# One layer of a YOCO trunk on one core: split products for the first two projections and the output projection, a paired block solve, 32 bytes of padding, and an inverse square root formed on DVE

## The chip, the cores and the metric

The kernel runs on one core of a Trainium2 chip. The metric is the device time of one execution in microseconds; a kernel's time is the median of its runs. TensorE is called PE, VectorE DVE, ScalarE ACT, GpSimd POOL, SyncE SP.

## The reference

One sequence of 512 tokens (S), width 1024 (D), float32 throughout. Layer 0 is an RWKV-7 mixer and a SwiGLU FFN, layer 1 differential attention with a shared K and V and a second FFN. Only the mixer's computation is touched by the change:

```python
h  = rms_norm(x, g_mix[0]);  hh = shift(h) - h
xr, xw, xk, xv, xa, xg = (h + hh * mu[i] for i in range(6))
r, k, v = xr @ w_r, xk @ w_k, xv @ w_v
w = -softplus(-(w0 + tanh(xw @ w1) @ w2)) - 0.5
a = sigmoid(a0 + (xa @ a1) @ a2);   g = sigmoid(xg @ g1) @ g2
kk = k * k_k, per head of 64:  kk / max(sqrt(sum(kk*kk)), 1e-12)
k  = k * (1 + (a - 1) * k_a)
# per head, over 512 tokens:
state = state * decay_t + (state @ -kk_t) (kk_t * a_t)^T + v_t k_t^T ;  y_t = state @ r_t
y  = groupnorm(y) * lnx_w + lnx_b + (sum(r*k*r_k)) * v
x  = x + (y * g) @ w_o
x  = x + (silu(gate) * up) @ w_down      # the FFN
```

## The kernel before

The residual stream is kept transposed: tiles of 128 features by 512 tokens. There are two ways to multiply in float32. `proj_f` gives float32 operands to PE as they are; such a product of 128x128 by 128x512 stands in the trace as two MATMUL records. `mm3` takes operands split into a high part (rounded to float32r by a copy on ACT) and a low part (the rest, a subtraction on DVE), and adds up three float32r products, high by high, high by low and low by high; each is one record. Before the change the mixer uses the first way and the two FFNs and the attention the second.

The mixer is cut into 16 heads, handled as 8 pairs in two halves of four (w = 0 and 1), and into 8 chunks of 64 tokens. It runs in this order.

- The opening merges four streams: the normalised input, the two low-rank projections w1 and a1 (`lora`, L339), and the first half of r (`r_half(0)`, L459 and L174). Each of them mixes its own input (`mix_tile`, L329): one ACT instruction at L335, one DVE instruction at L336, into a tile of tag `xm` that has two buffers; k's mixes go into `xk` and are kept for the second half. Weights come through `load_raw` into tag `wr`, which has three buffers, of which w1 and a1 hold two here.
- Then `k_half(0)` is drained alone.
- After that `plan` emits three streams in the order of planned times (the table TIMES: start, end and a bend of each). The first is `pairs(0)`, `solve(0)`, `rec(0)`; the second r, k, v, the gate and the output projection of half 0; the third `pairs(1)`, `solve(1)`, `rec(1)`. `plan` sets the order in which instructions are written down. [...]
- `pairs` begins with `norms` (L498): the sums of squares of the keys by PE (L507), a clamp on DVE (L512), `rsqrt` (L200: the power of minus one half on POOL at L206, then a Newton step of three DVE instructions, L208 to L210), a transpose on PE (L515) and a copy (L517). `pair_b` needs the result.
- `solve` (L660) inverts 64x64 triangular blocks: 31 steps of two DVE instructions (L673, L675), then the off-diagonal 32x32 blocks by PE: 16 products (L695), a copy on ACT (L696), 16 products (L699), a copy (L700), for two groups (q) by two heads (par) one after the other.
- `rec` runs the recurrence over 8 chunks (L724, L738, L766 on PE, copies and sums on DVE between them); the stream of projections fills PE meanwhile. `head_out` finishes each 128 tokens.
- The second half of the output projection, `out(1)`, is drained alone after the plan. Then the first FFN begins.

SBUF pools lie on a stack from the left; the pool `z` (six tiles of 8 KB per partition), and after it `xa` (eight tiles of 4 KB), lie at the right end. In the built program the tiles of `z` and `xa` begin 32 bytes past a multiple of 64 (`xa` at 196576, 200672 and so on), those of `xb`, `hid`, `xk`, `s` and `wr` at a multiple of 64. `xa` holds the moving operand of the first FFN's gate and up products and, later, of the attention's output projection; `xb` holds that of the second FFN. `s` is a tag of 13 tiles of 4 KB that most intermediate results of the mixer share.

Of the kernel before, what the change touches and what calls it, by code (L numbers as in the profile page):

```python
# [18 lines left out]
P = 128  # L19
D = 1024  # L20
S = 512
# [21 lines left out]
class Trunk:  # L43
# [3 lines left out]
                 gate=(153, 181, 1.0), out0=(181.0, 252.922016661, 1.25), pairs1=(65, 130, 1.0), solve1=(132.962208526, 188.90025602, 1.0))  # L47
# [138 lines left out]

    def proj_tok(self, W, xgen, evac):
# [12 lines left out]
    def rsqrt(self, out, m, tag="ty"):  # L200
# [9 lines left out]
        nc.vector.scalar_tensor_tensor(out=out, in0=z, scalar=1.5, in1=y, op0=ALU.add, op1=ALU.mult)  # L210

# [55 lines left out]
    def build(self):  # L267
        tc, nc, A = self.tc, self.nc, self.A
        self.tags = {}
        with ExitStack() as st:  # L270
# [16 lines left out]
            nc.vector.memset(self.mhalf, -0.5)  # L287
            banks = dict(ca=2, cb=2, pj=4)
# [170 lines left out]
    def r_half(self, w):  # L459
        for i in range(2):  # L460
            self.R[w * 2 + i] = self.T("s", [P, 2, S])
        return self.proj_f(self.A["w_r"], self.mixes("r", 0, w),
                           lambda o, ps: self.nc.scalar.copy(self.R[o // 2][:, o % 2, :], ps), gi=w)

    def k_half(self, w, kr):
        kr.extend(self.T("s", [P, 2, S]) for _ in range(2))
        return self.proj_f(self.A["w_k"], self.mixes("k", 2, w),
# [30 lines left out]
    def norms(self, q):  # L498
# [14 lines left out]
        self.rsqrt(inv[:, :, 0:8], m, "nv")  # L513
# [39 lines left out]
    def out_half(self, w, pg, x1):  # L553

        nc, A = self.nc, self.A
        yx = {}

        def ev(o, ps):
            yx[o] = self.T("xk", [P, S])
            nc.vector.tensor_tensor(out=yx[o], in0=ps, in1=self.oT[o // 2][:, o % 2, :], op=ALU.mult)  # L560
        self.lora2(pg, [A["g2a"], A["g2b"]], w, ev)
# [5 lines left out]
        for gi in range(2):  # L567
            yield from self.proj_f(A["w_o"], lambda kt: yx[kt], add, kts=range(w * 4, w * 4 + 4), gi=gi)
# [91 lines left out]
    def solve(self, w, Ld, N2):  # L660
# [28 lines left out]
        for q in range(2):  # L689
            ln = slice(q * 16, q * 16 + 16)  # L690
            for par in range(2):
                b0, b1 = slice(par * C, par * C + 32), slice(par * C + 32, par * C + 64)
                ps = self.bank("ca")
                for l in range(16):
                    nc.tensor.matmul(ps[b1, l * 32:l * 32 + 32], N2[b0, q * 16 + l, :], Td[b0, q * 16 + l, :], start=True, stop=True)  # L695
                nc.scalar.copy(Zt[b1, ln, :], ps[b1, :].rearrange("p (a b) -> p a b", a=16))  # L696
                ps2 = self.bank("cb")
                for l in range(16):
                    nc.tensor.matmul(ps2[b0, l * 32:l * 32 + 32], Zt[b1, q * 16 + l, :], Pd[b1, q * 16 + l, :], start=True, stop=True)  # L699
                nc.scalar.copy(Ps[q][b0, :, 32:64], ps2[b0, :].rearrange("p (a b) -> p a b", a=16))  # L700
                yield
# [465 lines left out]
```

## Time and profile before

| | |
|---|---|
| median of 3 runs | 1576.84 us (1575.41 to 1577.22) |
| the profiled execution | 1575.47 us, its span 1573.7 us |
| PE busy | 1501.3 us, 95% of the span |
| DVE, ACT, POOL busy | 729.5, 497.9, 219.5 us |
| mean granted PE clock | 0.98 |
| opening of the mixer (four merged streams) | about 27 to 83 us |
| k's first half | about 90 to 117 us |
| the plan | about 117 to 532 us |
| second half of the output projection | about 532 to 562 us |
| first FFN, attention, second FFN | about 562 to 1574 us |

The bounds of the stages are read from the order of PE's instructions in time. A busy PE is not a PE at its peak: records of matmuls overlap, so a rate is read from the distance of their starts.

### The profile page before, as it was taken

To read this page: it belongs to the slowest core of one execution; us is meant where nothing else is said; L and a number is where in the kernel's file an instruction comes from. 1 tells how busy PE (TensorE), PEld (TensorE's weight loads), DVE (VectorE), ACT (ScalarE), POOL (GpSimd) and SP (SyncE) were. 2 spreads that over 40 slices of the span, in tenths; PEclk is the share of its full clock that TensorE was granted. 3 is DMA by queue.
4 is the path that set the end of the run, shared out by engine and by line. 5 is a ranking of instruction groups with operands and counts; after the bars stand their busy time and mean duration, and the time that the engine had idled before them with its cause. 6 is when DMAs were issued, how large, how long until landed. Compare 5 with 4: busy or idle time off the path is not lost.

```text
span 1573.7 us, 22664 instructions
## 1 busy us (share of the span) xinstructions
PE 1501.3 (95%) x9448; PEld 1124.0 (71%) x9448; DVE 729.5 (46%) x1356; ACT 497.9 (32%) x881; POOL 219.5 (14%) x182
## 2 busy tenths in 40 slices
PE   3898998999999999999999998999999999999999
PEld 1244654666567468888888888988877888888887
DVE  6313638566423453343432357666666434434232
ACT  3332340212311142222221243356564333222211
POOL 0004313201201121111110003211101111111000
PEclk9999999999898999999999998999999999999999
DMA  3121432484420222222222231221011222222231
GB/s 113 41 87 57 169 130 91 162 294 163 170 95 20 77 95 94 94 94 94 95 94 94 98 108 68 92 70 43 29 51 68 99 103 94 94 101 100 95 120 67
DMA packets 51799, 154.21 MB, mean 98 GB/s; under 512 B 5488, under 2 KB 12016, under 8 KB 49648
## 3 DMA queue, kind: packets, MB, share of 16 engines
q1 hardware_dynamic: 50496, 151.18, 27.4%
q8 instruction: 74, 1.21, 0.3%
q10 hardware_dynamic: 1120, 1.32, 0.3%
q14 instruction: 29, 0.24, 0.1%
q0 software_dynamic: 80, 0.26, 0.0%
HBM read 131.77 MB, written 20.97 MB: 97 GB/s over the span
## 4 chain that ended last, share of the span: by engine, by line
PE 81%; DVE 9%; POOL 3%; issue 2%; ACT 2%; DMA 2%; ACTq 0%; SPq 0%; POOLq 0%; DVEq 0%
PE pj L158 12%; PE pj L157 12%; PE pj L156 12%; PE pj L182 10%; PE pj L195 2%; PE d L943 2%; PE d L945 2%; PE d L944 2%; PE cb L642 2%; PE cb L766 2%; PE ca L724 1%; POOL ty L206 1%; PE pj L363 1%; PE ca L157 1%; PE cb L157 1%
## 5 line engine op out<-in xcount | busy, mean ns | idle before, releaser
L150 ACT CAST wh<-wr 128x1024 fp32r<-128x1024 f32 x153 | 160.8, 1052 | 501.8 <-PE pj L157 226.2
L151 DVE TENSOR_TENSOR wl<-wr,wh 128x1024 fp32r<-128x1024 f32 x153 | 186.9, 1222 | 184.5 <-ACT wh L150 182.9
L156 PE MATMUL pj<-xa,wh 128*128 128x512 f32 x352 | 139.9, 397 | 1.0 <-ACT wh L150 1.0
L158 PE MATMUL pj<-xa,wl 128*128 128x512 f32 x352 | 139.6, 397 | 0.3 <-DVE wl L151 0.3
L157 PE MATMUL pj<-xa,wh 128*128 128x512 f32 x352 | 139.6, 397 | 0.0
L158 PE MATMUL pj<-xb,wl 128*128 128x512 f32 x352 | 137.1, 389 | 0.0
L156 PE MATMUL pj<-xb,wh 128*128 128x512 f32 x352 | 137.1, 389 | 0.0
L157 PE MATMUL pj<-xb,wh 128*128 128x512 f32 x352 | 137.0, 389 | 0.0
L833 POOL TENSOR_TENSOR hid<-ev,hid 128x512 fp32r<-128x512 f32 x44 | 68.1, 1548 | 405.5 <-ACT hid L832 405.5
L182 PE MATMUL pj<-xk,wr 128*128 128x512 f32 x256 | 123.8, 631 | 0.0
L829 DVE TENSOR_TENSOR ev<-pj,bc 128x512 f32<-128x512 f32 x44 | 30.4, 691 | 145.2 <-PE pj L158 145.2
L206 POOL TENSOR_TENSOR ty<-ty,mhalf 128x8 f32<-128x8 f32 (+1 forms) x28 | 47.6, 1699 | 306.0 <-DVE ty L782 150.0
L182 PEld LDWEIGHTS pj<-xk,wr 128*128 128x128 f32 x256 | 48.6, 199 | 53.8 <-issue 50.6
L826 DVE TENSOR_TENSOR ev<-pj,bc 128x512 f32<-128x512 f32 x44 | 30.4, 691 | 118.6 <-PE pj L158 116.1
L156 PEld LDWEIGHTS pj<-xa,wh 128*128 128x128 f32 x352 | 66.3, 188 | 18.2 <-ACT wh L150 2.2
L158 PEld LDWEIGHTS pj<-xa,wl 128*128 128x128 f32 x352 | 66.3, 188 | 16.8 <-DVE wl L151 0.7
L157 PEld LDWEIGHTS pj<-xa,wh 128*128 128x128 f32 x352 | 66.3, 188 | 16.0
L157 PEld LDWEIGHTS pj<-xb,wh 128*128 128x128 f32 x352 | 66.1, 188 | 13.9
L158 PEld LDWEIGHTS pj<-xb,wl 128*128 128x128 f32 x352 | 66.1, 188 | 13.7
L156 PEld LDWEIGHTS pj<-xb,wh 128*128 128x128 f32 x352 | 66.1, 188 | 13.6
L158 PE MATMUL pj<-hid,wl 128*128 128x512 f32 x176 | 68.5, 389 | 0.0
L156 PE MATMUL pj<-hid,wh 128*128 128x512 f32 x176 | 68.5, 389 | 0.0
(284 smaller groups left out, 2969.6 us busy)
## 6 DMA issues: line engine op xcount, KB each, us to landing
wr<-in_wgu SPq DMA_DIRECT2D x88, 512.0 KB, 3.5
wr<-in_wdn SPq DMA_DIRECT2D x44, 512.0 KB, 3.5
st_d<-z SPq DMA_DIRECT2D x16, 1024.0 KB, 4.7
z<-st_d SPq DMA_DIRECT2D x16, 1024.0 KB, 5.8
wr<-in_w_kv SPq DMA_DIRECT2D x16, 512.0 KB, 3.5
wr<-in_w_r SPq DMA_DIRECT2D x8, 512.0 KB, 3.5
wr<-in_w_k SPq DMA_DIRECT2D x8, 512.0 KB, 3.5
wr<-in_w_v SPq DMA_DIRECT2D x8, 512.0 KB, 3.5
```

Source lines behind the costliest of these rows:

```text
L150: nc.scalar.copy(hi, raw)
L151: nc.vector.tensor_tensor(out=lo, in0=raw, in1=hi.bitcast(F32), op=ALU.subtract)
L156: mm(out, wh, xh, start=start, stop=False)
L157: mm(out, wh, xl, start=False, stop=False)
L158: mm(out, wl, xh, start=False, stop=stop)
L182: self.nc.tensor.matmul(pss[i], w[:, kt % 2, i * P:i * P + P], x, start=kt == kts[0], stop=kt == kts[-1])
L195: self.nc.tensor.matmul(pss[tt], x[:, tt * P:(tt + 1) * P], w[:, kt % 2, :], start=kt == 0, stop=kt == KT - 1)
L206: nc.gpsimd.tensor_tensor(out=y, in0=m, in1=half.to_broadcast(shp), op=ALU.pow)
L642: nc.tensor.matmul(ps[f, o:o + P], BK[f, hf * 4 + c2 * 2 + c, u, :], Z[f, c2 * 2 + c, 0:2, :].rearrange("p a b -> p (a b)"), start=True, s ...
L766: nc.tensor.matmul(ps[o, i * C:(i + 1) * C], z[f, i, k, :], R[f, i, :], start=n == 0, stop=n == len(parts) - 1)
L833: nc.gpsimd.tensor_tensor(out=t[:, 1, :], in0=b, in1=t[:, 0, :].bitcast(F32), op=ALU.subtract)
L943: mm(ps[:, t], x[:, 0, :], hi, start=kt == 0, stop=False)
```

## The change

1. `r_half(0)` and `k_half(0)` go through a new function `proj_p`: weights and mixed inputs are split, into tiles of tag `z`, and multiplied with `mm3`. The second halves stay as they are.
2. `out_half` splits the gated output and the weights of w_o and uses `mm3`. The high parts take tiles of tag `s`, the low parts of tags `xk` and `wr`.
3. `norms` calls a new function `rsqrt_v`: a first guess from the bits by two DVE instructions and three Newton steps of three DVE instructions each; POOL's power is gone from there. `rsqrt` itself stays where else it is called.
4. The end of `solve` makes the products of both heads in turn within one loop, 32 to a bank, first all of L695's kind for q = 0 and 1, then all of L699's kind; of the two copies after each one goes to ACT and one to DVE.
5. In TIMES the gate moves from 153-181 to 172-190, and out0's start from 181.0 to 190.5.
6. A pool of 32 bytes is opened on the right before all others there, so `z` and `xa` begin 32 bytes lower.

```diff
--- before.py
+++ after.py
@@ -44,7 +44,7 @@
 
     TIMES = dict(pairs0=(-0.3, 60.1, 1.0), solve0=(60.8, 109.3, 0.8), rec0=(110, 180, 1.0), rec1=(194.0, 252.732477142, 1.0),
                  r1=(-4.9, 29.584587539, 1.0), k1=(30, 58.813540184, 0.9), v0=(60.0, 97.9, 1.0), v1=(99.712791157, 150.1, 1.0),
-                 gate=(153, 181, 1.0), out0=(181.0, 252.922016661, 1.25), pairs1=(65, 130, 1.0), solve1=(132.962208526, 188.90025602, 1.0))
+                 gate=(172, 190, 1.0), out0=(190.5, 252.922016661, 1.25), pairs1=(65, 130, 1.0), solve1=(132.962208526, 188.90025602, 1.0))
 
 
     START = 8, 7.5, 7.5, 8
@@ -184,6 +184,27 @@
                     evac(gi * 4 + i, pss[i])
             yield
 
+    def proj_p(self, W, xgen, evac, gi=0):
+
+        nc = self.nc
+        pss = [self.bank() for _ in range(4)]
+        for kt in range(KT):
+            if kt % 2 == 0:
+                w = self.load_raw(W[gi, kt // 2], [P, 2, 512])
+                wz, xz = (self.T("z", [P, 4, 512], F32R) for _ in range(2))
+                nc.scalar.copy(wz[:, 0:2, :], w)
+                nc.vector.tensor_tensor(out=wz[:, 2:4, :], in0=w, in1=wz[:, 0:2, :].bitcast(F32), op=ALU.subtract)
+            x = xgen(kt)
+            k = kt % 2
+            nc.scalar.copy(xz[:, k, :], x)
+            nc.vector.tensor_tensor(out=xz[:, 2 + k, :], in0=x, in1=xz[:, k, :].bitcast(F32), op=ALU.subtract)
+            for i in range(4):
+                c = slice(i * P, i * P + P)
+                self.mm3(pss[i], wz[:, k, c], wz[:, 2 + k, c], xz[:, k, :], xz[:, 2 + k, :], kt == 0, kt == KT - 1)
+                if kt == KT - 1:
+                    evac(gi * 4 + i, pss[i])
+            yield
+
     def proj_tok(self, W, xgen, evac):
 
         pss = [self.bank() for _ in range(NT)]
@@ -208,6 +229,20 @@
         nc.vector.tensor_tensor(out=z, in0=y, in1=y, op=ALU.mult)
         nc.vector.scalar_tensor_tensor(out=z, in0=z, scalar=-0.5, in1=m, op0=ALU.mult, op1=ALU.mult)
         nc.vector.scalar_tensor_tensor(out=out, in0=z, scalar=1.5, in1=y, op0=ALU.add, op1=ALU.mult)
+
+    def rsqrt_v(self, out, m, tag):
+
+        nc = self.nc
+        I32 = mybir.dt.int32
+        shp = list(m.shape)
+        y = self.T(tag, shp)
+        nc.vector.tensor_scalar(y.bitcast(I32), m.bitcast(I32), 1, None, op0=ALU.logical_shift_right)
+        nc.vector.tensor_scalar(y.bitcast(I32), y.bitcast(I32), -1.0, float(0x5F3759DF), op0=ALU.mult, op1=ALU.add)
+        z = self.T(tag, shp)
+        for i in range(3):
+            nc.vector.tensor_tensor(out=z, in0=y, in1=y, op=ALU.mult)
+            nc.vector.scalar_tensor_tensor(out=z, in0=z, scalar=-0.5, in1=m, op0=ALU.mult, op1=ALU.mult)
+            nc.vector.scalar_tensor_tensor(out=out if i == 2 else y, in0=z, scalar=1.5, in1=y, op0=ALU.add, op1=ALU.mult)
 
     def rows_bc(self, rstd, tag="ev"):
 
@@ -285,6 +320,8 @@
             nc.vector.memset(self.zero, 0.0)
             self.mhalf = cp.tile([P, 1], F32, name="mhalf")
             nc.vector.memset(self.mhalf, -0.5)
+            self.open(st, "pad", dict(pad=1), side="right")
+            self.T("pad", [P, 8])
             banks = dict(ca=2, cb=2, pj=4)
             with ExitStack() as ps:
                 self.open(ps, "ps0", banks, space=PSUM)
@@ -459,12 +496,12 @@
     def r_half(self, w):
         for i in range(2):
             self.R[w * 2 + i] = self.T("s", [P, 2, S])
-        return self.proj_f(self.A["w_r"], self.mixes("r", 0, w),
+        return (self.proj_f if w else self.proj_p)(self.A["w_r"], self.mixes("r", 0, w),
                            lambda o, ps: self.nc.scalar.copy(self.R[o // 2][:, o % 2, :], ps), gi=w)
 
     def k_half(self, w, kr):
         kr.extend(self.T("s", [P, 2, S]) for _ in range(2))
-        return self.proj_f(self.A["w_k"], self.mixes("k", 2, w),
+        return (self.proj_f if w else self.proj_p)(self.A["w_k"], self.mixes("k", 2, w),
                            lambda o, ps: self.nc.scalar.copy(kr[o // 2 - 2 * w][:, o % 2, :], ps), gi=w)
 
     def v_half(self, w):
@@ -510,7 +547,7 @@
         nc.gpsimd.memset(inv, 0.0)
         m = self.T("nv", [P, 4, 8])
         nc.vector.tensor_scalar(m, ps[:, 0:32].rearrange("p (a b) -> p a b", a=4), 1e-24, None, op0=ALU.max)
-        self.rsqrt(inv[:, :, 0:8], m, "nv")
+        self.rsqrt_v(inv[:, :, 0:8], m, "nv")
         pt = self.bank("cb")
         nc.tensor.transpose(pt[:, 0:P], inv.rearrange("p a b -> p (a b)"), self.ident)
         it = self.T("it", [P, P])
@@ -553,11 +590,17 @@
     def out_half(self, w, pg, x1):
 
         nc, A = self.nc, self.A
-        yx = {}
+        yx, yh, yl = {}, {}, {}
 
         def ev(o, ps):
             yx[o] = self.T("xk", [P, S])
             nc.vector.tensor_tensor(out=yx[o], in0=ps, in1=self.oT[o // 2][:, o % 2, :], op=ALU.mult)
+            if o % 2 == 0:
+                yh[o // 2] = self.T("s", [P, 2, S], F32R)
+            h = yh[o // 2][:, o % 2, :]
+            nc.scalar.copy(h, yx[o])
+            yl[o] = self.T("xk", [P, S], F32R)
+            nc.vector.tensor_tensor(out=yl[o], in0=yx[o], in1=h.bitcast(F32), op=ALU.subtract)
         self.lora2(pg, [A["g2a"], A["g2b"]], w, ev)
         yield
 
@@ -565,7 +608,20 @@
             v = x1[o // 2][:, o % 2, :]
             nc.vector.tensor_tensor(out=v, in0=ps, in1=v, op=ALU.add)
         for gi in range(2):
-            yield from self.proj_f(A["w_o"], lambda kt: yx[kt], add, kts=range(w * 4, w * 4 + 4), gi=gi)
+            pss = [self.bank() for _ in range(4)]
+            for kt in range(w * 4, w * 4 + 4):
+                k = kt % 2
+                if k == 0:
+                    W = self.load_raw(A["w_o"][gi, kt // 2], [P, 2, 512])
+                    wh, wl = self.T("s", [P, 2, 512], F32R), self.T("wr", [P, 2, 512], F32R)
+                    nc.scalar.copy(wh, W)
+                    nc.vector.tensor_tensor(out=wl, in0=W, in1=wh.bitcast(F32), op=ALU.subtract)
+                for i in range(4):
+                    c = slice(i * P, i * P + P)
+                    self.mm3(pss[i], wh[:, k, c], wl[:, k, c], yh[kt // 2][:, k, :], yl[kt], k == 0 and kt % 4 == 0, kt % 4 == 3)
+                    if kt % 4 == 3:
+                        add(gi * 4 + i, pss[i])
+                yield
 
     def done_list(self, tiles):
         for j in range(KT):
@@ -686,19 +742,27 @@
                                         self.cst[:, C_RM + b:C_RM + b + 1], None, op0=ALU.mult)
             Ps.append(pt)
         Zt = self.T("s", [P, 32, 32])
-        for q in range(2):
-            ln = slice(q * 16, q * 16 + 16)
-            for par in range(2):
-                b0, b1 = slice(par * C, par * C + 32), slice(par * C + 32, par * C + 64)
-                ps = self.bank("ca")
-                for l in range(16):
+        B = [[slice(par * C + b * 32, par * C + b * 32 + 32) for par in range(2)] for b in range(2)]
+        v = lambda t: t.rearrange("p (a b) -> p a b", a=16)
+
+        def first(q):
+            ps = self.bank("ca")
+            for l in range(16):
+                for b0, b1 in zip(*B):
                     nc.tensor.matmul(ps[b1, l * 32:l * 32 + 32], N2[b0, q * 16 + l, :], Td[b0, q * 16 + l, :], start=True, stop=True)
-                nc.scalar.copy(Zt[b1, ln, :], ps[b1, :].rearrange("p (a b) -> p a b", a=16))
-                ps2 = self.bank("cb")
-                for l in range(16):
-                    nc.tensor.matmul(ps2[b0, l * 32:l * 32 + 32], Zt[b1, q * 16 + l, :], Pd[b1, q * 16 + l, :], start=True, stop=True)
-                nc.scalar.copy(Ps[q][b0, :, 32:64], ps2[b0, :].rearrange("p (a b) -> p a b", a=16))
-                yield
+            for b1, copy in zip(B[1], (nc.scalar.copy, nc.vector.tensor_copy)):
+                copy(Zt[b1, q * 16:q * 16 + 16, :], v(ps[b1, :]))
+
+        def second(q):
+            ps = self.bank("cb")
+            for l in range(16):
+                for b0, b1 in zip(*B):
+                    nc.tensor.matmul(ps[b0, l * 32:l * 32 + 32], Zt[b1, q * 16 + l, :], Pd[b1, q * 16 + l, :], start=True, stop=True)
+            for b0, copy in zip(B[0], (nc.scalar.copy, nc.vector.tensor_copy)):
+                copy(Ps[q][b0, :, 32:64], v(ps[b0, :]))
+        for f, q in ((first, 0), (first, 1), (second, 0), (second, 1)):
+            f(q)
+            yield
         self.Pt[w] = Ps
 
     def clear(self, ps):
```

## The prediction

> **What bounds the kernel now.** I read the page first, then the chain that ended last, the stretches of the mixer, and then PE's instructions in time, stage by stage.
>
> ```profile
> L150 ACT CAST wh<-wr 128x1024 fp32r<-128x1024 f32 x153 | 160.8, 1052 | 501.8 <-PE pj L157 226.2
> L151 DVE TENSOR_TENSOR wl<-wr,wh 128x1024 fp32r<-128x1024 f32 x153 | 186.9, 1222 | 184.5 <-ACT wh L150 182.9
> ```
>
> Splitting one weight tile costs ACT 1.05 us and DVE 1.22 us. In the stretches, the columns after each window are busy time with counts in the order PE, weight load, DVE, ACT, POOL, then the granted clock:
>
> ```profile
> 27.00:83.00 56.00, 47.83 (x97) 15.51 (x98) 27.05 (x40) 24.39 (x38) 0.00 (x0) 1.00 0.10 33
> 240.00:260.00 20.00, 17.42 (x81) 9.60 (x81) 18.64 (x39) 1.52 (x3) 7.45 (x9) 0.91 0.10 35
> 334.00:440.00 106.00, 102.69 (x1258) 64.68 (x1255) 62.03 (x151) 28.07 (x58) 17.83 (x20) 0.92 0.51 177
> 420.00:440.00 20.00, 20.00 (x239) 13.48 (x239) 3.92 (x6) 5.48 (x11) 2.37 (x4) 0.58 0.14 54
> ```
>
> PE sets the pace nearly everywhere in the plan (102.69 of 106 us); the opening (47.83 of 56) and the stretch around 240 us, where DVE is at 18.64 of 20, are the exceptions. So PE time taken out of the plan mostly comes off the end, and PE's gaps are worth closing. ACT is below half everywhere. At 420 to 440 us PE is busy without a gap and yet the clock is 0.58.
>
> **The price of a product.** Both ways of multiplying are in the trace; the first and the last of 29 and of 32 starts in a row for two moving operands, and the whole of k's first half:
>
> ```profile
> 699.33 0.39 PE L156 MATMUL pj<-xa,wh 128*128 128x512 f32 x1
> 705.89 0.39 PE L157 MATMUL pj<-xa,wh 128*128 128x512 f32 x1
> ...
> 1294.80 0.39 PE L158 MATMUL pj<-xb,wl 128*128 128x512 f32 x1
> 1301.83 0.39 PE L156 MATMUL pj<-xb,wh 128*128 128x512 f32 x1
> ...
> 89.82 27.73 PE L182 MATMUL pj<-xk,wr 128*128 128x512 f32 x64
> ```
>
> From start to start a float32r record takes 6.56/28 = 0.234 us with xa and 7.03/31 = 0.227 us with xb. A split product is three of these, 0.68 us from an operand like xb. A float32 product is two records, 27.7/32 = 0.87 us when they run dense; between other work it is 0.91 us (four in 3.67 us, in the rows of the opening below). Each of the 128 products that are converted saves 0.19 to 0.23 us of PE.
>
> **The opening (r's first half).** The rows of one pair of steps, and the wait for the weights from the chain:
>
> ```profile
> 52.55 0.72 ACT L335 ACTIVATE xm<-x,omu 128x512 f32<-128x512 f32 x1 [2.91 <-PE pj L182]
> 53.30 0.75 DVE L336 SCALAR_TENSOR_TENSOR xm<-x,par,xm 128x511 f32<-128x511 f32 x1 [2.88 <-ACT xm L335]
> 56.11 3.67 PE L182 MATMUL pj<-xm,wr 128*128 128x512 f32 x8 [0.93 <-DMA wr<-in_w_r]
> 59.82 0.72 ACT L335 ACTIVATE xm<-x,omu 128x512 f32<-128x512 f32 x1 [3.88 <-PE pj L182]
> 61.38 1.07 PE L347 MATMUL cb<-xm,wr 128*64 128x512 f32 x2 [0.60 <-DVE xm L336]
> 66.13 0.72 ACT L335 ACTIVATE xm<-x,omu 128x512 f32<-128x512 f32 x1 [2.91 <-PE pj L182]
> ...
> 52.54 3.44 DMA wr<-in_w_r
> ...
> L832 ACT CAST hid<-ev 128x512 fp32r<-128x512 f32 x44 | 27.4, 622 | 30.1 <-DVE ev L830 30.1
> L830 DVE TENSOR_TENSOR ev<-ev,ev 128x512 f32<-128x512 f32 x44 | 30.4, 692 | 4.4
> ```
>
> Two steps take 66.13 - 52.55 = 13.58 us, 6.79 each; 7.27 where the next weight must land first (it has one tile of wr to land in), 6.31 where not. After the change the weight tile is given back once it is split, so the load of 3.44 us starts a pair earlier and hides. But r's input now takes four instructions before PE has both parts: mix 0.72 and 0.75, copy 0.62, subtraction 0.69, with the handovers about 3.0 us. It still needs one of the two xm tiles, which w's product, queued on PE behind r's, gives back. In the present order (r, w, a) a step is then r's 12 records, 2.72 us, w's product 1.07 (as a's in L347's row), and the 3.0 us less 0.2 because the first records need only the high part: 6.6 us, a gain of 8 x 0.2 = 1.6 us. If w's and a's products are placed ahead of r's, PE's 2.72 + 2.14 us plus some waiting make 5.1 us, a gain of 13. I take **4 us** (0 to 13): nearest to the order the trace has.
>
> **k's first half** is drained alone and dense: 27.73 us become 96 x 0.227 = 21.8. Per step DVE has 0.75 + 0.69 + 0.61 and ACT 0.72 + 0.62 + 0.53 us, both under PE's 2.72, and most mixes for it are done during the opening. Gain **6 us** (5 to 6).
>
> **The norms.** The two places, on PE, POOL and DVE:
>
> ```profile
> 124.31 3.68 PE L182 MATMUL pj<-xm,wr 128*128 128x512 f32 x8
> 132.99 0.31 PE L515 MATMUL cb<-cst,iv 128*128 128x128 f32 x1 [5.00 <-POOL Dc L603]
> 133.56 5.17 PE L182 MATMUL pj<-xm,wr 128*128 128x512 f32 x8 [0.26 <-DVE xm L336]
> ...
> 124.76 5.42 POOL L206 TENSOR_TENSOR nv<-nv,mhalf 128x32 f32<-128x32 f32 x1 [1.57 <-DVE nv L512]
> 130.14 1.26 POOL L606 TENSOR_TENSOR b<-pr,pr 128x512 f32<-128x512 f32 x1
> 131.48 1.32 POOL L607 TENSOR_TENSOR pr<-pr,s 128x512 f32<-128x512 f32 x1
> ...
> 130.21 1.24 DVE L208 TENSOR_TENSOR nv<-nv 128x32 f32<-128x32 f32 x1 [5.53 <-POOL nv L206]
> 131.48 0.19 DVE L209 SCALAR_TENSOR_TENSOR nv<-nv,nv 128x32 f32<-128x32 f32 x1
> 131.71 1.14 DVE L210 SCALAR_TENSOR_TENSOR iv<-nv,nv 128x32 f32<-128x32 f32 x1
> ...
> 240.05 0.19 DVE L208 TENSOR_TENSOR nv<-nv 128x32 f32<-128x32 f32 x1 [4.70 <-POOL nv L206]
> ...
> 242.18 0.30 PE L515 MATMUL cb<-cst,iv 128*128 128x128 f32 x1 [4.34 <-DVE iv L210]
> 242.31 5.29 PE L195 MATMUL pj<-wr,xk 128*128 128x512 f32 x8
> ```
>
> Removed: POOL's 5.42 us and three DVE instructions. Added: 11 small DVE instructions; by the start-to-start of L209 and L210 (131.48 to 131.71) each costs 0.23 us, 2.5 us together. Begun at 124.7 they end at 127.2, before PE's eight records end at 128.0, so the gap of 5.00 + 0.26 us goes; so does the slow group behind it (5.17 against 3.68 us, 1.5). That is 6.7 us; I take 6.5. At 234 us DVE carries `solve`'s steps as well, so the 11 cost 2.5 us plus about 2 of interleaved steps, and the gap of 4.34 shrinks to about 1; with the slow group (1.6) and the 4.70 us in which DVE itself stood behind POOL, less the added DVE work, I take 4. Together **10.5 us** (6 to 12). Late next is PE's own queue, which I take to be full.
>
> [...]
>
> **The block solve.** Last products of the first solve, two full groups and a stretch in which two kinds ran together:
>
> ```profile
> 293.35 2.11 PE L695 MATMUL ca<-s,s 32*32 32x32 f32 x64
> ...
> 299.49 0.19 PE L695 MATMUL ca<-s,s 32*32 32x32 f32 x1
> 299.49 0.19 PE L699 MATMUL cb<-s,s 32*32 32x32 f32 x1
> 299.52 0.19 PE L695 MATMUL ca<-s,s 32*32 32x32 f32 x1
> 299.52 0.19 PE L699 MATMUL cb<-s,s 32*32 32x32 f32 x1
> ...
> 303.62 3.31 PE L699 MATMUL cb<-s,s 32*32 32x32 f32 x64
> ```
>
> A run of 64 records on one part of the array takes 2.11 us for L695 and 3.31 for L699; where two parts alternate, two records start every 0.03 us. With the two heads in turn, 64 records could take half: 1.05 and 1.65 us saved per group, two groups and two solves, 11 us at most. The waits for copies are filled by projections already. I take about half, **6 us** (0 to 11). [...]
>
> **out0 and the gate.** 32 products give PE 7 us. Against it stand four split weights (1.05 + 1.22 us) and four split outputs (0.62 + 0.69 us), 6.7 us on ACT and 7.6 on DVE, in DVE's queue between the recurrence's short copies, which PE waits for. The gate's 16 products (15 us) leave the recurrence of half 0 and stand beside `solve(1)`; that recurrence then has less fill. I take **2 us** (-8 to 7).
>
> **out1** runs alone:
>
> ```profile
> 534.39 27.54 PE L182 MATMUL pj<-xk,wr 128*128 128x512 f32 x62
> ```
>
> Its 32 products, 28.5 us at this rate, become 21.8; the first input waits 1.3 us more for its split, which nothing covers. Gain **5.5 us** (3 to 7).
>
> **The padding.** The records with xa moving are 0.0075 us apart from those with xb, with the same kinds of work beside them. xa is 32 bytes off a multiple of 64 and xb is not. The first FFN's 3 x 352 and the attention output's 192 records, 1248 x 0.0075 = 9.4 us: **9.5 us** (0 to 10). Nothing else in the FFNs and the attention changes.
>
> **The sum**: 4 + 6 + 10.5 + 6 + 2 + 5.5 + 9.5 = 43.5 us, off the profiled execution's 1575.47 us, which is 1.4 below the median of 1576.84: **1532 us**.
>
> **The rivals.** *The recurrences keep the time.* The vector engines and the two xm tiles pace the opening and the new splits stand in the recurrence's way: opening 0, norms 6, solve 0, out0 -8, out1 3, k 5, padding 9.5, together 15.5 us, 1560. For it speaks DVE at 18.64 of 20 us around 240; against it PE's 95% in the plan.
>
> *The padding does nothing*, because xa's rate comes from where it lies and not from the 32 bytes: 34 us, 1541.5. Against it: the rate is the same in all of xa's eight tiles and in both its users.
>
> *The Newton steps meet POOL*: nine instructions at up to 1.2 us are 10.8 us at each place, longer than the 8.1 us from L206's start to L210's end that they replace. The 10.5 us go and some 5 are lost: 1547.5.
>
> *Slower.* PE's clock: 420 to 440 us has clock 0.58 with PE busy throughout, on small products. The gate's dense products no longer stand in the recurrence of half 0; if its small products let the clock fall to one half from 360 to 440 us, 80 us of PE work become up to 160, less the 8 lost there now, and about 50 of it stays after idle time: 1532 + 50 = 1582. It decides from 44 us on. Against it: the other recurrence products hold 0.92.
>
> **How the numbers follow.** The forecast has 0.62, the paced case 0.17, the padding 0.11, the port 0.05, the clock 0.05. The forecast's own range is 1517 to 1546. The range is 1508 to 1559: from all terms near their best (66 us, 1509) to the paced case. A measurement of this kernel can tell about 0.2% (3 us) from no change; only the clock case, and several misses at once, end there or beyond: faster 0.94, same 0.01, slower 0.05.
>
> **What would show it.** Records with xa at 0.227 us (padding). k's first half at 22 us and no wait for in_w_r in the chain. L515 without PE idle before it, and eight records behind it in 3.7 us. L695 and L699 in groups of 64 at half their time. About 22 us of split products at the end of the mixer. Wrong it would be if idle time on PE before L733's, L743's and L754's users grew, or if the clock between 340 and 440 us were clearly under 0.92.

## The result, and the profile after

The changed kernel took 1528.51 us (median of 4 runs, 1523.91 to 1535.6) against 1576.24 us (4 runs, 1575.41 to 1577.22): the ratio is 0.970, 95% interval 0.966 to 0.974, 48 us less. The profiled execution is the slowest of the four, 1535.6 us. The head of its page:

```profile
span 1533.8 us, 23005 instructions
PE 1461.6 (95%) x9576; PEld 1133.6 (74%) x9576; DVE 766.8 (50%) x1420; ACT 521.4 (34%) x913; POOL 210.7 (14%) x180
```

PE is still the bound: its busy time fell by 39.7 us and the span by 39.9. By the starts of PE's marking instructions in the two profiled executions (us from one mark to the next) the 39.9 us lie here:

| stretch, up to | before | after | less |
|---|---|---|---|
| end of the opening (first L363/L400) | 82.8 | 76.6 | 6.2 |
| first sums of the key norms (L507/L544) | 38.0 | 33.0 | 5.0 |
| first transpose of the norms (L515/L552) | 12.2 | 8.7 | 3.5 |
| second group of L363/L400 | 86.8 | 84.7 | 2.1 |
| second transpose of the norms | 22.4 | 19.6 | 2.8 |
| start of the first recurrence | 71.6 | 62.1 | 9.5 |
| last group of L363/L400 (both recurrences, second `solve`, gate, out0) | 204.1 | 196.1 | 8.0 |
| first FFN | 44.8 | 45.8 | -1.0 |
| second FFN | 645.2 | 641.4 | 3.8 |
| end | 365.8 | 365.8 | 0.0 |

The two recurrences stand in one row because their border is not the same place in both kernels: PE's first products of the second recurrence come after the second `solve` before (440.65 us) and ahead of its last products now (386.02).

The four executions of the changed kernel differ by 11.7 us, and their granted clocks tell why: 0.983, 0.988, 0.991 and 0.990 for 1535.6, 1530.04, 1523.91 and 1526.97 us. Span times mean clock (below: the *net* time, an estimate that counts all of the span as PE's) is 1508 to 1510 in all four. For the kernel before it is about 1540 (1573.7 x 0.980 = 1542 in its profiled execution; 1537 to 1544 in the 33 others that ran beside the experiments). So 31 to 35 of the 48 us are work and waits, and the other 13 to 17 are clock, which the sum of the prediction did not have. Why the changed kernel is granted more clock (0.978 to 0.991 in seven executions, against 0.971 to 0.982) is not shown. The estimate is coarse: it halves waits for other engines, too, where the clock is at one half, within one kernel it varied by up to 11 us, and one execution of the kernel before showed a clock of 0.935 at 1579.32 us, where it fails. One execution of the changed kernel, in the last experiment, took 8103 us at a clock of 1.00; it is in no median, ratio or range here, and nothing on record explains it.

Now the rows that answer to those of the prediction, PE's instructions in time (start, duration; in brackets the idle time before and its releaser). The opening:

```profile
52.92 1.19 PE L156 MATMUL pj<-z,z 128*128 128x512 f32 x4 [1.39 <-ACT z L199]
55.91 1.07 PE L384 MATMUL ca<-xm,wr 128*64 128x512 f32 x2
56.82 1.02 PE L384 MATMUL cb<-xm,wr 128*64 128x512 f32 x2
59.23 1.19 PE L156 MATMUL pj<-z,z 128*128 128x512 f32 x4 [1.39 <-ACT z L199]
...
84.09 1.09 PE L156 MATMUL pj<-z,z 128*128 128x512 f32 x3 [0.33 <-ACT z L199]
...
106.12 3.60 PE L182 MATMUL pj<-xm,wr 128*128 128x512 f32 x8
```

A step takes 6.31 us, with 1.39 us of waiting for the high part of r's input, and no wait for in_w_r. k's first half stands between 84.09 and 106.12: 22.03 us for 96 records. The norms, on PE, DVE and POOL:

```profile
109.55 3.63 PE L544 MATMUL cb<-cst,pr 128*128 128x2 f32 x32
113.04 5.38 PE L182 MATMUL pj<-xm,wr 128*128 128x512 f32 x8
118.25 0.27 PE L552 MATMUL cb<-cst,iv 128*128 128x128 f32 x1
118.36 1.02 PE L182 MATMUL pj<-xm,wr 128*128 128x512 f32 x2
...
113.22 0.19 DVE L549 TENSOR_SCALAR nv<-cb 128x32 f32<-128x32 f32 x1 [7.63 <-PE cb L544]
113.44 1.07 DVE L239 TENSOR_SCALAR nv<-nv 128x32 int32<-128x32 int32 x1
114.55 0.18 DVE L240 TENSOR_SCALAR nv<-nv 128x32 int32<-128x32 int32 x1
...
117.33 0.18 DVE L245 SCALAR_TENSOR_TENSOR iv<-nv,nv 128x32 f32<-128x32 f32 x1
...
113.21 1.26 POOL L663 TENSOR_TENSOR pr<-pr,s 128x512 f32<-128x512 f32 x1
...
222.62 0.27 PE L552 MATMUL cb<-cst,iv 128*128 128x128 f32 x1
```

Neither transpose waits here. From the clamp (113.22) to the last Newton step's end (117.51) are 4.3 us, inside the eight records of PE. One of the eleven steps, the first, met POOL. There is still a slow group of eight records (5.38 us), now ahead of the transpose: from 113.9 to 117.3 us the granted clock was 0.50. In the other profiled execution of the same kernel (the last experiment) that stretch has a clock of 1.00, the group takes 3.68 us, and the transpose waits 0.93 us for DVE:

```profile
113.83 3.68 PE L182 MATMUL pj<-xm,wr 128*128 128x512 f32 x8
118.44 0.30 PE L552 MATMUL cb<-cst,iv 128*128 128x128 f32 x1 [0.93 <-DVE iv L245]
```

So the slow group goes with the clock of the one execution and not with the kernel.

The end of `solve`:

```profile
270.28 2.21 PE L752 MATMUL ca<-s,s 32*32 32x32 f32 x128
272.42 3.70 PE L216 MATMUL pj<-wr,xk 128*128 128x512 f32 x8
275.96 0.95 PE L657 MATMUL cb<-rkc,pr 128*128 128x2 f32 x8
276.84 2.21 PE L760 MATMUL cb<-s,s 32*32 32x32 f32 x128
```

Now 128 records take 2.21 us, where 64 of L695's kind took 2.11 and 64 of L699's 3.31. The beginning of out(1), on PE and then on ACT:

```profile
500.54 0.79 PE L156 MATMUL pj<-s,s 128*128 128x512 f32 x1 [4.00 <-ACT s L617]
...
505.63 0.63 PE L158 MATMUL pj<-s,wr 128*128 128x512 f32 x1
506.06 0.58 PE L156 MATMUL pj<-s,s 128*128 128x512 f32 x1
506.47 0.40 PE L157 MATMUL pj<-xk,s 128*128 128x512 f32 x1
506.71 0.40 PE L158 MATMUL pj<-s,wr 128*128 128x512 f32 x1
...
498.92 0.62 ACT L601 CAST s<-xk 128x512 fp32r<-128x512 f32 x1 [1.36 <-DVE xk L597]
499.45 1.04 ACT L617 CAST s<-wr 128x1024 fp32r<-128x1024 f32 x1
```

PE stands for 4.00 us until the first weights of w_o are split, since that copy (L617) is queued on ACT behind the output's own copies (L601). Then the records start 0.43 us apart for 5.5 us, and 0.24 at 506.47. These two eat what the split saves. Last, the clock in the stretch in which the second `solve` ends (columns as in the prediction's stretches):

```profile
386.00:390.00 4.00, 2.79 (x84) 2.19 (x83) 1.58 (x3) 1.23 (x4) 1.25 (x3) 1.00 0.68 217
390.00:394.00 4.00, 4.00 (x11) 1.09 (x9) 0.69 (x1) 1.17 (x3) 0.00 (x0) 0.55 0.00 0
394.00:398.00 4.00, 4.00 (x68) 2.36 (x67) 2.07 (x3) 1.20 (x2) 0.00 (x0) 0.50 0.01 4
398.00:402.00 4.00, 4.00 (x5) 0.99 (x5) 1.28 (x2) 0.62 (x1) 0.00 (x0) 0.50 0.00 0
```

After 4 us of 64x64 and 32x32 products with waits of at most 1.22 us (386 to 390) the clock falls to one half, and it stays there although PE is busy without a gap: twelve records of L400 that follow take 12.09 us. The small products alone do not decide it. With the output projection undone (an experiment below) the same rows follow the same wait of 1.22 us, the clock stays at 1.00, and the twelve records take 6.39 us:

```profile
390.60 0.33 PE L846 MATMUL cb<-cst,ho 128*128 128x128 f32 x1 [1.22 <-DVE ho L841]
...
396.14 6.39 PE L400 MATMUL pj<-s,wr 128*128 128x512 f32 x12
```

### The profile page after: what moved, and what is told of

The parts are those of the page before. It is cut to its first block, busy times and chain, and to the rows that moved or that the text cites. A ratio compares the mean times of both kernels' runs of the same rounds, so it can differ in the third digit from the quotient of the medians.

```text
span 1533.8 us, 23005 instructions
## 1 busy us (share of the span) xinstructions
PE 1461.6 (95%) x9576; PEld 1133.6 (74%) x9576; DVE 766.8 (50%) x1420; ACT 521.4 (34%) x913; POOL 210.7 (14%) x180
## 4 chain that ended last, share of the span: by engine, by line
PE 82%; DVE 8%; ACT 3%; POOL 3%; issue 2%; DMA 1%; ACTq 0%; SPq 0%; POOLq 0%; DVEq 0%
PE pj L156 15%; PE pj L157 14%; PE pj L158 14%; PE pj L182 3%; PE pj L216 3%; PE d L1007 3%; PE d L1009 2%; PE d L1008 2%; PE cb L698 2%; PE ca L788 2%; PE cb L830 2%; POOL ty L227 2%; PE pj L400 2%; PE a L1105 1%; PE ca L158 1%
## 5 line engine op out<-in xcount | busy, mean ns | idle before, releaser
L156 PE MATMUL pj<-hid,wh 128*128 128x512 f32 x176 | 68.5, 389 | 0.0
L157 PE MATMUL pj<-hid,wh 128*128 128x512 f32 x176 | 68.5, 389 | 0.0
L216 PE MATMUL pj<-wr,xk 128*128 128x512 f32 x128 | 61.8, 622 | 0.0
```

Of the source, the lines that this page charges most:

```text
L156: mm(out, wh, xh, start=start, stop=False)
L157: mm(out, wh, xl, start=False, stop=False)
L216: self.nc.tensor.matmul(pss[tt], x[:, tt * P:(tt + 1) * P], w[:, kt % 2, :], start=kt == 0, stop=kt == KT - 1)
```

## The experiments

In each, the kernel before ran beside it on the same chip. Times are medians. The changed kernel itself ran at other times and mostly on other chips, so an experiment is set against it by net times (about 1509 for the changed kernel), which are good to a few us, and by the rows of a stage.

**The norms alone** (the kernel before, with `rsqrt_v` in `norms` and nothing else).

```diff
-        self.rsqrt(inv[:, :, 0:8], m, "nv")
+        self.rsqrt_v(inv[:, :, 0:8], m, "nv")
```

> The kernel before with one edit: the key norms' inverse square root by the new DVE function. My theory (PE's gap behind the POOL power goes, and the slow group behind it): 10.5 us faster than before (6 to 12), the gaps of 5.0 and 4.3 us ahead of the norms' transposes gone or under 1 us. Rival (the gap is only moved: later work in the same stretch waits for POOL, or the Newton steps stand behind POOL): 0 to 3 us.

1570.99 us against 1575.71, ratio 0.996 (0.994 to 0.998), 10 runs. PE's rows:

```profile
122.04 3.90 PE L521 MATMUL cb<-cst,pr 128*128 128x2 f32 x32
125.80 5.09 PE L182 MATMUL pj<-xm,wr 128*128 128x512 f32 x8
130.73 0.27 PE L529 MATMUL cb<-cst,iv 128*128 128x128 f32 x1
```

From sums to transpose 8.7 us (12.2 before), and 17.7 for the second place (219.1 to 236.8). The stretch behind the first transpose, up to the second group of L363's kind, takes 84.8 us, as in the changed kernel, against 86.8 before, so these 2 us are the norms' as well. The net time is 1532, 8 less than before; the time fell by 5 to 6 only, as the clock was lower (0.972 to 0.981 in the ten runs).

**The norms undone** (the changed kernel with POOL's power).

```diff
-        self.rsqrt_v(inv[:, :, 0:8], m, "nv")
+        self.rsqrt(inv[:, :, 0:8], m, "nv")
```

> The changed kernel with one edit: the norms back on the POOL power. If the parts simply add, it is slower than the changed kernel by what the same edit gains on the kernel before, about 10 us, so some 38 us faster than before. Rival (in the changed kernel the stretch is set by other things, such as DVE's triangular steps): only 3 to 5 us slower than the changed kernel.

1545.43 us, ratio 0.981 (0.977 to 0.985): 17 us above the changed kernel, of which about 6 are net (1515; 1509 to 1520). The wait is back whole:

```profile
122.76 0.30 PE L552 MATMUL cb<-cst,iv 128*128 128x128 f32 x1 [5.00 <-POOL Dc L659]
```

So the step is worth 6 to 8 us of work. The rest of the 17 comes and goes with the clock (0.973 to 0.988 in these four runs).

**160 bytes of padding in place of 32.**

```diff
-            self.T("pad", [P, 8])
+            self.T("pad", [P, 40])
```

> The changed kernel with 160 bytes of padding in place of 32; xa then has the same remainder by 512 as the weight tiles of the FFN (320). The padding of 32 bytes brought xa's records from 0.2343 to only 0.2324 us, not to 0.2267. Theory A (the remainder of the moving operand against the weights decides): xa's records at 0.227 us, the first FFN and the attention's output projection 7 us shorter. Theory B (only the multiple of 64 counts, the rest is another thing): 0.232 us as before, no change.

1522.27 us (one run; net 1504, 5 less than the changed kernel). Records with xa moving, first and last of 32 in a row, in the changed kernel, here, and with 96 bytes (the next experiment):

```profile
654.70 0.39 PE L156 MATMUL pj<-xa,wh 128*128 128x512 f32 x1
...
661.90 0.40 PE L157 MATMUL pj<-xa,wh 128*128 128x512 f32 x1
```

```profile
654.77 0.39 PE L158 MATMUL pj<-xa,wl 128*128 128x512 f32 x1
...
661.80 0.39 PE L156 MATMUL pj<-xa,wh 128*128 128x512 f32 x1
```

```profile
654.83 0.39 PE L157 MATMUL pj<-xa,wh 128*128 128x512 f32 x1
...
661.92 0.39 PE L158 MATMUL pj<-xa,wl 128*128 128x512 f32 x1
```

Over 31 distances: 0.2323 us in the changed kernel, 0.2268 here, 0.2287 with 96 bytes. FFN0's gate and up products, up to the first product with hid, took 242.8 us, 248.7 in the changed kernel, 251.2 before: 8.4 us less than before.

**96 bytes of padding**, to tell a step from a slope.

```diff
-            self.T("pad", [P, 8])
+            self.T("pad", [P, 24])
```

> The changed kernel with 96 bytes of padding: a multiple of 64, with another remainder by 128, 256 and 512 than in the changed kernel. Theory A (remainder against the weights): still above 0.230 us, perhaps another value. Theory B (only the multiple of 64): 0.2324 us exactly as in the changed kernel.

1532.69 us (one run, clock 0.981, net 1502; as one run each, the nets of 1504 and 1502 do not rank the two paddings, and the rates do). With the distance between the begin of xa's tiles and that of the weight tiles in the built programs, taken modulo 512 bytes (the author's choice; taken modulo 256 the four are the same), the four kernels make a series: 0 bytes 0.227 us (160 bytes of padding), 64 bytes 0.229 (96), 128 bytes 0.232 (32, the change), 160 bytes 0.234 (before). It is a slope, not the step at a multiple of 64 that the prediction assumed.

In these four kernels only xa moves and the weights stay, so its distance from them is not told apart from its own place. k's first half in the changed kernel and the two padding experiments tells them apart: there both operands lie in `z`, at distance 0, and move together. From the first to the last start its 96 records took 21.79, 21.84 and 21.82 us with 32, 160 and 96 bytes, so with both moved together the place made no more than 0.05 us of difference. Distance is not the whole rule either: with the norms undone, at the same places as in the changed kernel, the records of the first FFN came 0.233 us apart and not 0.232.

**The end of `solve` undone** (the changed kernel with before's loop; one line of it shown).

```diff
-        for f, q in ((first, 0), (first, 1), (second, 0), (second, 1)):
...
+        for q in range(2):
```

> The changed kernel with the end of the block solve as before (16 products, a copy, 16 products, a copy, head by head). My theory (two parts of the array in turn take half the time, gain 6 us, at most 11): 6 us slower than the changed kernel, so some 42 us faster than the kernel before; the groups of 64 records back at 2.1 to 3.3 us. Rival (the projections between the products hide it): no slower than the changed kernel.

1543.73 us, ratio 0.976 (0.973 to 0.979), net 1515, 6 more. The first recurrence begins at 292.2 instead of 284.7. The groups of 64 take their old times again:

```profile
271.66 2.11 PE L751 MATMUL ca<-s,s 32*32 32x32 f32 x64
...
281.94 3.37 PE L755 MATMUL cb<-s,s 32*32 32x32 f32 x64
```

**The output projection undone** (float32 products for w_o, both halves, at the new times).

```diff
-            pss = [self.bank() for _ in range(4)]
...
+            yield from self.proj_f(A["w_o"], lambda kt: yx[kt], add, kts=range(w * 4, w * 4 + 4), gi=gi)
```

> The changed kernel with the output projection unsplit, as before. My theory, mended by the trace of the changed kernel: the second half gained nothing there (PE waits 4.0 us for the first weight split and then runs six us at half clock), the first half some 5 us within the recurrence; so 3 to 6 us slower than the changed kernel in the recurrence and the same from the last block of head sums to the first FFN. Rival (as predicted): 7.5 us slower, 5.5 of it at the end.

1539.38 us, ratio 0.972 (0.968 to 0.977), net 1518, 9 more. From the last group of L400 to the first FFN it took 44.9 us (478.0 to 522.9) against 45.8, so in time the split half 1 is worth nothing. In net it is worth some 2.5 us: the clock of that stretch was 0.92 here and 0.85 in the changed kernel (net 41.5 against 39.0). The other 6.5 come from the half that runs inside the second recurrence: from the start of the first recurrence to the last group of L400 it took 190.6 us at a clock of 1.00, against 196.1 at 0.94 (net 184.1).

**The old times of gate and out0.**

```diff
-                 gate=(172, 190, 1.0), out0=(190.5, 252.922016661, 1.25), ...
+                 gate=(153, 181, 1.0), out0=(181.0, 252.922016661, 1.25), ...
```

> The changed kernel with the gate and out0 at their old planned times. My theory: the move is worth little by itself (0 to 3 us either way). Rival (the gate's products beside the solve are what keeps PE filled there): 5 us or more slower than the changed kernel. Second rival (the move brings the stretch at half clock around 390 to 410 us): 5 us or more faster, with a higher mean clock.

1536.45 us, ratio 0.971 (0.967 to 0.974); net 1507, 2 less than the changed kernel, the clock 0.981 to 0.984. The move by itself gains nothing; if anything it costs 2 us.

**r's first half undone** (float32 products in the opening).

```diff
-        return (self.proj_f if w else self.proj_p)(self.A["w_r"], self.mixes("r", 0, w),
+        return self.proj_f(self.A["w_r"], self.mixes("r", 0, w),
```

> The changed kernel with r's first half as before (float32 products). My theory, from the two traces: the opening ends some 6 us later (82.8 against 76.6 us there), the rest is the same: 5 to 7 us slower than the changed kernel. Rival (k's first half loses too, since its splits are no longer prepared during the opening): 8 us or more.

1541.74 us (2 runs), ratio 0.977 (0.974 to 0.979). The opening ends at 83.3 instead of 76.6, and the first sums of the norms begin 6.4 us later (116.0). The net time is only about 2 more (1511), but the trace shows no loss of the 6.4 us within the plan. At the last group of L400 this execution stands at 481.8 us, 10.2 of them lost to half clock (net 471.6), the changed kernel at 480.8 with 15.4 lost (465.4): still 6.2 apart. What closes the gap is the stretch from there to the first FFN, which ran at a clock of 0.70 here (52.0 us) and 0.85 there (45.8), and in which the net counts PE's waits at half.

**The two misses mended** (`e_best` in the texts below): 160 bytes of padding, and in `out_half` the first pair of w_o is loaded and split ahead of the gate's second product.

```diff
+        ready = split(0, w * 4)
         self.lora2(pg, [A["g2a"], A["g2b"]], w, ev)
...
-                    W = self.load_raw(A["w_o"][gi, kt // 2], [P, 2, 512])
...
+                    wh, wl = ready or split(gi, kt)
+                    ready = None
```

> The changed kernel with 160 bytes of padding, and in the output projection the first weight pair loaded and split ahead of the low-rank product. My theory: 5.5 us (padding: 1248 records by 4.5 to 5.7 ns) and 4 to 6 us at the end of the mixer (no wait of 4.0 us for the weight split, less time at half clock); some 1517 us, ratio 0.962 to 0.965. Rival (PE's idle time before the output projection is the last head sums' and stays, and with it the low clock): 6 us from the padding alone.

1527.2 us (1518.04 to 1536.19), ratio 0.965 (0.959 to 0.971), net 1497 to 1503. From the last group of L400 to the first FFN 40.9 us at a clock of 0.92, 5 less than the changed kernel's 45.8 at 0.85, of which some 3 are clock; out(1)'s first product no longer waits for its weights:

```profile
491.01 0.80 PE L156 MATMUL pj<-s,s 128*128 128x512 f32 x1
```

Net it is 8 to 9 us better than the changed kernel, but its median is not told apart from it: 18 us of spread, at clocks of 0.977 to 0.991.

**Dense products against the fall of the clock** (`e_warm`): the same kernel, and eight bf16 products of 128x128 by 128x512 ahead of each L760 group of the second `solve`. Their results are overwritten.

```diff
             ps = self.bank("cb")
+            for _ in range(8 * w):
+                nc.tensor.matmul(ps, self.ones.bitcast(BF)[:, 0:P], self.scanm.bitcast(BF)[:, 0:512], start=True, stop=True)
```

> The kernel of e_best with 16 added bf16 products of 128x128 by 128x512, whose results are overwritten: eight ahead of each group of L760's kind in the second block solve, where the clock falls. They cost 16 x 0.22 = 3.5 us of PE at full clock. Theory 1 (the clock falls because the array sees only small products there and little is done between them): the granted clock from 380 to 420 us rises from 0.76 to 0.88 to over 0.9, span times mean clock 2 to 4 us up, and the spread of the runs shrinks: 1518 to 1522 us. Theory 2 (the clock falls for a reason outside this stretch, or comes back only after long dense work): the clock stays, and the time is 3 to 5 us more than e_best's.

1520.07 us (1517.61 to 1520.46), ratio 0.962 (0.9605 to 0.964). The stretches from 380 to 420 us in the changed kernel, with the two misses mended, and here:

```profile
380.00:400.00 20.00, 18.32 (x170) 7.23 (x168) 6.98 (x15) 6.56 (x12) 4.19 (x5) 0.76 0.21 65
400.00:420.00 20.00, 20.00 (x127) 11.63 (x128) 7.42 (x11) 4.22 (x6) 0.00 (x0) 0.64 0.17 56
```

```profile
380.00:400.00 20.00, 17.76 (x193) 9.01 (x191) 8.18 (x14) 7.13 (x13) 4.20 (x5) 0.76 0.19 64
400.00:420.00 20.00, 20.00 (x179) 12.68 (x179) 9.74 (x16) 5.21 (x8) 0.00 (x0) 0.98 0.25 78
```

```profile
380.00:400.00 20.00, 17.81 (x239) 8.17 (x238) 9.45 (x16) 8.78 (x16) 4.20 (x5) 1.00 0.27 91
400.00:420.00 20.00, 20.00 (x212) 13.00 (x211) 9.95 (x17) 5.20 (x8) 0.00 (x0) 1.00 0.24 70
```

In the profiled execution the clock stays at 1.00 through the place where it fell; in all four runs the mean is 0.992 or 0.993, and the spread shrinks from 18 to 2.9 us. The added products came 0.22 us apart (six of them from 389.88 to 391.18). It costs some 6 us net (1504 to 1508) and more than wins it back: the median is 7 us lower than without, though the two intervals overlap. Against the kernel as changed (0.966 to 0.974) they do not: this version is the fastest of those run. That the added products are what holds the clock is likely and not proven. The next experiment, which has them too, shows 0.992 in all four runs; but `e_best`, with 0.977 to 0.991, ran on another chip, and in single executions without them (160 bytes of padding; the output projection undone) the clock did not fall at this place either.

**Dense products at the last transposes as well** (twelve more, behind the second product of the gate in half 1).

```diff
         self.lora2(pg, [A["g2a"], A["g2b"]], w, ev)
+        if w:
+            ps = self.bank("ca")
+            for _ in range(12):
+                nc.tensor.matmul(ps, self.ones.bitcast(BF)[:, 0:P], self.scanm.bitcast(BF)[:, 0:512], start=True, stop=True)
```

> The kernel of e_warm with twelve more products of the same kind, results unused, at the last transposes of the second half, where PE waits for the last head sums and the clock falls once more (3.4 us lost between 480 and 500 us). Theory (the clock follows the work that the array is given): the loss at 480 to 500 us goes, 2 to 3 us faster than e_warm, about 1517 us, ratio 0.960 to 0.962. Rival (the added products delay the transposes that the end waits for, by three times 0.2 us each, and the clock gives no more than that back): the same as e_warm within 1 us.

1521.15 us, ratio 0.9635 (0.961 to 0.966): no gain.

```profile
490.35 0.45 PE L876 MATMUL cb<-cst,ho 128*128 128x128 f32 x1 [1.98 <-DVE ho L871]
490.59 1.49 PE L615 MATMUL ca<-cst,ones 128*128 128x512 bf16 x3
```

The added products came behind the wait of 1.98 us and themselves ran 0.43 us apart (three from 490.59 to 491.87), where those of the experiment before had been 0.22 apart; out(1) behind them went at 0.23 us from its second record on (496.29), and the loss of 3.4 us between 480 and 500 us was the same.

**The changed kernel once more.**

> The changed kernel once more, beside the kernels of this call on one chip. All theories: as measured, 1524 to 1536 us, ratio 0.966 to 0.974, with a spread of some 10 us that goes with the mean clock; span times mean clock 1508 to 1510 us.

Ratio 0.971 (0.966 to 0.975); 1528.66, 1536.44 and 1542.76 us at clocks of 0.989, 0.982 and 0.978, net 1507 to 1510 as expected, the times in part above the expected 1524 to 1536. The same program thus runs anywhere from 1524 to 1543 us, and the clock says where.

## Why the prediction was right, and where it was not

The time came within 4 us of the forecast, but by misses that cancel: the sum took 43.5 us off at an unchanged clock, the work fell by 31 to 35, and the clock, on which the sum did not count, gave the other 13 to 17. So close a hit is luck. The parts below, at their places or from the reversals, come to 6.2 + 5.7 + 8.4 + 6 + 4 + 2.4 + 2.8 = 35.5 us.

*The opening* (4 us predicted, 6.2 measured at its place). The order r, w, a and the wait for the copy came as described; the step takes 6.31 us, as before's step did where no weight had to land, and 6.6 was estimated. For that order the prediction's own working gave 1.6 us; the 4 was a choice between two orders, and came nearer by luck. The gain holds through the plan: in the reversal the last group of L400 is still 6.2 us later, net, which bears out the prediction's first step ("PE time taken out of the plan mostly comes off the end").

*k's first half* (6; 5.7 measured: 22.03 us). Right at its place; no run undid it alone.

*The norms* (10.5; 8.4 measured: 6.3 between sums and transposes and 2.1 behind the first transpose; 8 net alone, 6 undone). The mechanism was right, and the size some 2 us too large. Both gaps went. The eleven DVE steps took 4.3 us at the first place, where 2.5 were estimated, and in this execution a slow group remained ahead of the first transpose (5.38 us), which the prediction had going with the gap (1.5 us); it did not remain in the other profiled execution. The rival in which the Newton steps meet POOL (the 0.05 called the port) was wrong in size. Its 1.2 us for a step is what L208 (1.24 us beside L606) and L210 (1.14 beside L607) took in the kernel before; here none of the Newton steps met POOL, which was rid of the power and had done L662 and L663 by 114.47. The one step it touched was the shift L239: it took 1.07 us, until L663 was done, and 0.18 in the execution with 96 bytes of padding, where it began 0.1 us ahead of L663's end; at the second place of the profiled execution (217.88), with L663 done at 217.64, it took 0.17. What held these three instructions beside POOL is not shown.

*The block solve* (6; 6 net in the reversal, 7.5 at its place). Right. Two groups of 64 took 4.22 us (L695) and 6.62 (L699) and take 2.21 each now, 6.4 us less in the first `solve`. If the second saves as much it is 12.8 us of records, more than the upper bound of 11; the reversal shows 6 of it at the end.

*out0 and the gate* (2, from -8 to 7). The reversals say 6.5 for the split within the recurrence and some -2 for the move, about 4 together: inside the range. The new copies on ACT and DVE did not hold the recurrence. PE's waits ahead of the same 448 records of the second recurrence (445.7 to 517.8 us before, 409.3 to 480.7 after; group, busy, mean, idle before), before and then after:

```profile
L724 PE MATMUL ca<-rs,z 64*64 64x64 f32 x448 | 19.4, 230 | 0.9 <-DVE rs L754 0.9
```

```profile
L788 PE MATMUL ca<-rs,z 64*64 64x64 f32 x448 | 18.9, 225 | 0.6 <-DVE rs L807 0.5
```

They did not grow, and from the start of the first recurrence to the last group of L400 the time fell by 8.0 us, about 2 of them clock (0.93 before, 0.94 after).

*out1* (5.5; -1.0 measured in time, 2.4 in net). This step failed. The prediction charged 1.3 us for the first split input and left out that the weight's copy queues on ACT behind the output's own copies: 4.00 us of idle PE, and then 5.5 us of records at half clock, about 2.7 us lost (from 500.54 to 506.06 twelve distances in 5.52 us, in place of 12 x 0.23). Mended, 5 us came back, some 3 of them clock.

*The padding* (9.5; 2.5 in FFN0, predicted 1056 x 0.0075 = 7.9 there; some 2.8 with the attention's output projection). This step failed by its mechanism. "xa is 32 bytes off a multiple of 64 and xb is not" was true and not the cause. What counts in the four kernels is how far the moving tile lies from the weights modulo 512 bytes; xb lay at distance 0. The 32 bytes moved xa from 160 to 128: 0.0019 us of 0.0075. The price of the gap was right: with xa at distance 0 FFN0 fell by 8.4 us. The rival that the rate "comes from where it lies and not from the 32 bytes" (0.11) came nearer to the truth for this term.

*The clock* (not in the sum; as a rival -50 us, 0.05). Its condition was met in part: between 340 and 440 us the clock was 0.88 in the profiled execution, below the 0.92 named as a sign of error, and 12 us were lost there. Those are losses that the kernel before had too (8.4 us at 420 to 440), so they did not decide. What makes the clock fall and come back is not shown: with eight dense products ahead of each group it stayed at 1.00 at this place, and without them it stayed there in some executions and not in others. At out(1) it came back after 5.5 us of work (500.54 to 506.06); but between 394 and 408 us PE was busy without a gap, on records of full size at the end, and the clock stayed at one half (0.50) for all of it.

## What to carry to other kernels

A saving that rests on split operands begins with the split: look at what the first split weight is queued behind, and emit it a stage earlier. When runs of one kernel differ by a per cent, look at the granted clock before looking at the work, and judge small edits by the stage's own rows; span times clock is good to a few us, and less where waits fall into half clock. A difference in rate between two operands was here a question of where both tiles lie (0.227 to 0.234 us), so test two or three places before naming the rule.

## What the runs showed of the hardware

- The start-to-start time of float32r records of 128x512 rose with the distance of the moving tile from the weight tile, modulo 512 bytes: 0.227 us at 0, 0.229 at 64, 0.232 at 128 (0.233 in one kernel), 0.234 at 160; modulo 256 the distances are the same. Where both tiles moved together (96 records of k's first half, three places) the time stayed within 0.05 us of 21.8. Why is not known, and distances above 160 were not tried.
- Two parts of the array fed in turn took 128 records of 32x32 products in 2.21 us, 17 ns each, in the changed kernel; one part alone took 33 ns (2.11 us for 64 records) or 52 ns (3.31 us for 64) in the kernel before.
- In a stretch of 4 us of 64x64 and 32x32 products with waits of at most 1.22 us the clock fell to one half in one execution of the changed kernel, which lost 12 us; over the same rows in another kernel it stayed at 1.00. With 16 dense bf16 products among them, about 4 us of PE time, the mean clock was 0.992 or 0.993 in eight executions of eight; without them, in `e_best`, it was 0.977 to 0.991 in four.
- In the clock records of the traces, the stretches at one half that end within the span last 3.41 us or a whole multiple of it: four of 3.41 us, three of 6.83, one of 10.24 and one of 17.07 in the kernel before, 3.41 (two), 6.83, 13.65 and 23.89 us in the changed kernel, 30.72 us in its other profiled execution.
- A DVE shift of 128x32 took 1.07 us beside a POOL instruction (L239 from 113.44, L663 until 114.47, in the changed kernel), 0.18 us where that was about to end (96 bytes of padding) and 0.17 us with POOL idle (217.88 in the changed kernel).
